# A depthwise convolution in blocks of 32 outputs from 64 inputs, with eight channels side by side in the array, and the key projection moved to the end

## The chip, the cores and the metric

The kernel runs on one core of a Trainium2 chip. The metric is the device time of one execution in microseconds. The kernel before takes 2551.14 us (the median of 3 runs, 2549.97 to 2555.72). A TensorE (PE), a VectorE (DVE), a ScalarE (ACT) and a GpSimd (POOL) compute; SyncE (SP) issues every DMA.

## The reference

The kernel computes a trunk of two layers on x of 1024 tokens by 1024 channels in fp32. Each layer projects x to 9 blocks of 256 columns that feed four mixers, joins the mixers' outputs by an output projection and a LayerNorm, and runs a SwiGLU network with a second LayerNorm. The change touches the first mixer and the order of the last three blocks.

```python
for l in range(2):
    h = x @ w_in[l]                                 # 1024 -> 9 * 256 columns
    a, g = split(h[:, 0:512])                       # mixer A: 256 channels
    z = a * sigmoid(g)
    z = depthwise_conv(z, conf_dw_w[l])             # 31 taps along the tokens, centred
    y_a = silu(layer_norm(z + conf_dw_b[l], conf_ln_g[l], conf_ln_b[l]))
    y_b = s5(h[:, 512:768])                         # mixer B: a state-space scan
    y_c = gate * conv3(c * v)                       # mixer C: h[:, 768:1536]
    q, k, v = split(h[:, 1536:2304])                # mixer D: 4 heads, two softmax maps each
    y_d = diff_attention(rope(q), rope(k), v)
    x = layer_norm(1.414 * x + concat(y_a, y_b, y_c, y_d) @ w_out[l])
    x = layer_norm(1.414 * x + swiglu(x))
```

## The kernel before

**Large matmuls.** Each fp32 product is made of three fp32r products, a high and a low half of both operands (`mm3`). In a layer, blocks of w_in go through a ring of two tiles (`win`); `load_in_block` loads one and splits it. Channel-major blocks are made by `chan_gemm` (tile `cg`), token-major ones by `tok_gemm` (tile `tg`). The nine blocks go in the order of `in_blocks` (line 1513): S5 input, a, g, three for mixer C, then keys, values, queries.

**The convolution.** `conf_a` and `conf_g` leave z channel-major in `zp`. `conv_windows` (line 1068) transposes windows of 128 inputs that step by 96, 11 of them, so that tokens stand on partitions (`zT`, tile `convz`; transposes `cvw`). For each of the 256 channels `conv_part` (line 1083) does one fp32 matmul (`cvo`): 128 inputs on the rows, the channel's 128x96 band of taps as weights, its 11 windows as the moving columns. The bands are read from a table in DRAM (`taps_scr`), nine channels at a time, into a ring of three buffers. DVE adds the bias. `conv_norm` (line 1103) takes mean and variance with `bn_stats`, normalizes, transposes back (`cvb`) and applies gain, bias and SiLU on ACT.

The parts stand among the eight `s5_pair` steps (line 1560). A pair puts eight matmuls (`s5v`) before a chain of DVE operations and six (`s5y`) after it; its tables need matmuls `s5wp` and `s5k`. Mixer C's blocks are spread between the pairs as a list `gem`.

**Attention.** `attn_k` (line 1187) copies a token pair's keys to SBUF (ACT), applies the rotation (POOL, six operations), stacks high and low halves (ACT cast, POOL subtraction), transposes them (`ktp`, eight per token block of 128) and copies them to `kst`. `attn_heads` computes the scores (`sc`) of a query block against all 1024 keys, so the first `sc` needs every `kst`; DVE takes the row's maximum, ACT the exponentials. The four tiles of w_out are split at that time too.

**Order.** Nothing runs in program order. `Weaver` records all operations and sorts them with a list scheduler: it has a cost per operation, a shift in priority per step and layer (`SHIFT`, line 73), and a preference among engines for the operations that may run on any of two or three (`PREF`, line 86). The result is one order per engine, in which that engine then waits in turn. In a profile every operation stands under line 471 (`emit`), so tiles tell them apart. An fp32 matmul that is not a transpose leaves two records on PE, so the 512 convolution matmuls are 1024 records.

Of the kernel before, what the change touches and what calls it, by code (L numbers as in the profile page):

```python
# [9 lines left out]
F32 = mybir.dt.float32  # L10
# [8 lines left out]
P = 128  # L19
# [5 lines left out]
GW = 256  # L25
# [20 lines left out]
R_SW, R_LG, R_LB, R_GB, NROW = 0, 3, 4, 5, 6  # L46


CB, CWIN, NBLK, CG = 96, 128, 11, 9
NCK = -(-GW // CG)  # L50
WROW = CB + CWIN
CBANK = 43
# [16 lines left out]
class Weaver:  # L69
# [3 lines left out]
    SHIFT = {"None": -3232, "attn_finish0": 525, "attn_finish1": -8000, "attn_heads0": 2951, "attn_heads1": -4395,  # L73
# [12 lines left out]
    PREF = {"attn_finish0 gpsimd": -4310, "attn_finish0 scalar": -769, "attn_finish0 vector": 4528,  # L86
# [398 lines left out]
class Trunk:  # L485
# [3 lines left out]
    def __init__(self, ctx, tc, t):  # L489
# [16 lines left out]
        self.ident = self.identr.bitcast(F32)  # L506
        self.mhalf = self.cp.tile([P, 6], F32, name="mhalf")
        nc.vector.memset(self.mhalf, -0.5)
        self.rope = self.cp.tile([P, NJ, 2, 4], F32, name="rope_sb")
        nc.sync.dma_start(self.rope, t["rope"])  # L510


# [1207 lines left out]
```

## Time and profile before

| what | value |
|---|---|
| runs, median of 3 | 2551.14 us (2549.97 to 2555.72) |
| the profiled execution, own time | 2548.31 us |
| its span, first to last instruction | 2546.5 us |
| mean granted TensorE clock | 0.964 of full |
| PE, DVE, POOL, ACT busy | 2438.0, 1592.5, 1243.4, 795.2 us |

The profile gives each engine's busy time and, where an engine was idle, what ended the wait. "PEclk" is the share of full clock that TensorE was granted; in this trace a stretch is at full clock or at half of it (2.4 or 1.2 GHz), and a mean between them is a mix of the two. The mean duration of a matmul is longer than its share of the time, since matmuls overlap; busy time divided by the count is the share.

### The profile page before, as it was taken

The numbers are of one execution on the slowest core, as the hardware profiler recorded it, in microseconds if no ns is written. First come the engines' busy times: TensorE is split into PE (matmuls) and PEld (weight loads), VectorE is DVE, ScalarE is ACT, GpSimd is POOL, SyncE is SP. The second block draws the span as 40 slices with busy tenths as digits, with TensorE's granted clock in tenths as the row PEclk, the third lists the DMA queues.
The fourth block names the chain that finished last, engine by engine and source line by source line (L and its number), as shares of the span: only waits on it lengthen the run. The fifth ranks groups of instructions, "written<-read, shape, count | busy, mean of one in ns | idle before, by whom it ended". The sixth has DMA issues, their size and how long they took to land. (4 is left out here: it accounts for less than half of the span.)

```text
span 2546.5 us, 34450 instructions
## 1 busy us (share of the span) xinstructions
PE 2438.0 (96%) x13464; PEld 2049.7 (80%) x13464; DVE 1592.5 (63%) x2559; ACT 795.2 (31%) x1343; POOL 1243.4 (49%) x1015
## 2 busy tenths in 40 slices
PE   8999989888999999999899999899989999999997
PEld 7889987677888888888688899777778888888885
DVE  6688348886555555555563785698855445554456
ACT  2200356543222222222231113555432222222231
POOL 2201373535566666565640004745376655555574
PEclk9998899999999999999899989999999999999998
DMA  6334321114111111111333342211241111111212
GB/s 165 100 90 132 98 73 51 60 51 155 53 53 55 50 50 58 51 53 55 113 114 85 85 124 91 73 63 55 72 132 58 53 56 52 56 50 50 58 53 96
DMA packets 193081, 193.53 MB, mean 76 GB/s; under 512 B 84878, under 2 KB 168088, under 8 KB 192664
## 3 DMA queue, kind: packets, MB, share of 16 engines
q1 hardware_dynamic: 192920, 191.34, 24.9%
q8 instruction: 106, 1.74, 0.3%
q14 instruction: 55, 0.45, 0.1%
HBM read 164.61 MB, written 26.71 MB: 75 GB/s over the span
## 5 line engine op out<-in xcount | busy, mean ns | idle before, releaser
L471 PE MATMUL up<-xT,wring 128*128 128x512 f32 x2112 | 485.9, 389 | 0.0
L471 PEld LDWEIGHTS up<-xT,wring 128*128 128x128 f32 x2112 | 396.4, 188 | 82.3
L471 PE MATMUL dn<-wring,g 128*128 128x512 f32 x1920 | 450.4, 391 | 3.9 <-POOL wring L471 3.1
L471 POOL TENSOR_TENSOR wring<-upraw,wring 128x512 fp32r<-128x512 f32 x220 | 311.5, 1418 | 250.4 <-ACT wring L471 250.1
L471 PEld LDWEIGHTS dn<-wring,g 128*128 128x128 f32 x1920 | 359.8, 188 | 83.3 <-POOL wring L471 6.6
L471 PE MATMUL up<-xB,wring 128*128 128x512 f32 x1584 | 370.0, 389 | 0.2 <-DVE xT L471 0.2
L471 PEld LDWEIGHTS up<-xB,wring 128*128 128x128 f32 x1584 | 297.3, 188 | 62.1 <-DVE xT L471 0.4
L471 DVE TENSOR_TENSOR r<-r,dn 128x512 f32<-128x512 f32 x288 | 197.9, 687 | 214.0 <-PE dn L471 214.0
L471 ACT CAST wring<-upraw 128x512 fp32r<-128x512 f32 x220 | 136.6, 621 | 469.8 <-PE dn L471 162.5
L471 PE MATMUL cg<-xh,win 128*128 128x512 f32 x640 | 220.9, 414 | 3.1 <-POOL win L471 1.9
L471 PE MATMUL tg<-win,xh 128*128 128x256 f32 x1024 | 203.0, 296 | 1.0 <-POOL win L471 0.6
L471 PE MATMUL wo<-wout,yhl 128*128 128x512 f32 x768 | 195.8, 400 | 0.0
L471 PEld LDWEIGHTS tg<-win,xh 128*128 128x128 f32 x1024 | 170.5, 202 | 3.2 <-POOL win L471 0.9
L471 ACT ACTIVATE probs<-sc,asm 128x1024 f32<-128x1024 f32 x128 | 143.2, 1120 | 91.8 <-DVE asm L471 91.7
L471 DVE TENSOR_REDUCE asm<-sc 128x1 f32<-128x1024 f32 x128 | 155.3, 1217 | 24.7 <-PE sc L471 24.3
L471 PEld LDWEIGHTS wo<-wout,yhl 128*128 128x128 f32 x768 | 142.1, 190 | 28.8 <-POOL yhl L471 0.3
L471 POOL TENSOR_TENSOR wring<-w2raw,wring 128x512 fp32r<-128x512 f32 x80 | 103.7, 1301 | 105.0 <-ACT wring L471 105.0
L471 PE MATMUL tg<-win,xl 128*128 128x256 f32 x512 | 153.2, 300 | 0.0
L471 PEld LDWEIGHTS cg<-xh,win 128*128 128x128 f32 x640 | 126.0, 197 | 32.7 <-issue 2.9
L471 POOL CAST win<-wraw 128x1024 fp32r<-128x1024 f32 x21 | 27.8, 1326 | 212.6 <-PE cg L471 160.1
L471 PE MATMUL cg<-xl,win 128*128 128x512 f32 x320 | 129.5, 405 | 0.0
L471 POOL TENSOR_TENSOR wring<-tw,wring 128x512 fp32r<-128x512 f32 x88 | 122.7, 1394 | 7.8 <-ACT wring L471 7.8
(232 smaller groups left out, 3851.1 us busy)
## 6 DMA issues: line engine op xcount, KB each, us to landing
upraw<-in_w_ffn_dram SPq DMA_DIRECT2D x88, 512.0 KB, 3.8
w2raw<-in_w_ffn_dram SPq DMA_DIRECT2D x44, 512.0 KB, 3.5
wraw<-in_w_in_dram SPq DMA_DIRECT2D x36, 512.0 KB, 4.5
ctap<-taps_scr SPq DMA_DIRECT2D x38, 432.0 KB, 4.9
woraw<-in_w_out_dram SPq DMA_DIRECT2D x16, 512.0 KB, 3.7
r<-x_scr SPq DMA_DIRECT2D x16, 512.0 KB, 4.0
conv<-taps_scr SPq DMA_DIRECT2D x18, 432.0 KB, 4.8
x_scr<-xr SPq DMA_DIRECT2D x14, 512.0 KB, 3.0
```

The source lines that it names most:

```text
L471: getattr(e, method)(*args, **kwargs)
```

## The change

The convolution uses 32 blocks of 32 outputs, each from a window of 64 inputs. Windows of 128 inputs are still transposed, now stepping by 32, and each transpose serves two windows, one on the lower and one on the upper 64 partitions: channels 0 to 63 of a half take the lower rows, 64 to 127 the upper. A channel's matmul has its 64x32 windows as weights and its 64x32 band of taps as moving operand; row half and output column group go round so that eight matmuls in a row take eight places of the array. The taps of 64 channels are read by two DMAs into one buffer, four times per layer. Channels then lie in four groups of 32 partitions per output time, so mean and variance are sums over the free axis followed by a small matmul with a matrix of ones per group (`grp4`), and the transposes back go two output times at a time. `conv_norm` is recorded inside the S5 loop at pair 3. The blocks run values, queries, keys. `SHIFT` and `PREF` have other numbers throughout; two lines of 21 are shown.

```diff
-CB, CWIN, NBLK, CG = 96, 128, 11, 9
+CB, CWIN, NBLK, WROW = 32, 64, 32, 96
...
-            "short_v0": -2551, "short_v1": -1049, "to_xT0": -2061, "token_operands0": 5395, "token_operands1": 2148}
+            "short_v1": 7832, "to_xT0": -5018, "token_operands0": 5383, "token_operands1": 1484}
...
-            pair = int(outs[0].shape[0]) == 64
-            return max(128.0, 0.4167 * 4 * n + 5) * (0.57 if pair else 1.0), 0
+            k, m = int(kw["lhsT"].shape[0]), int(outs[0].shape[0])
+            if k == 64 and m == 32:
+                return 40.0, 0
+            return max(128.0, 0.4167 * 4 * n + 5) * (0.57 if m == 64 else 1.0), 0
...
+        for w0 in range(-2, NBLK, 4):
+            ps = self.b((P, 4, P), "cvw")
+            for i in range(min(4, NBLK - w0)):
+                c0, c1 = CB * (w0 + i), min(CB * (w0 + i) + P, 1040)
+                if c0 < 0:
+                    nc.tensor.matmul(ps[64:P, i, :], lhsT=z[:, c0 + 64:c1], rhs=self.ident, start=True, stop=True)
+                else:
+                    self.tr(ps[0:c1 - c0, i, :], z[:, c0:c1])
+            for h in range(2):
...
+                        nc.scalar.copy(zt[64 * h:64 * h + n, :, x0:x1].rearrange("p c b -> p b c"), src[0:n, i0:i0 + x1 - x0, :])
...
-            for c in range(c0, c1):
-                q, k = divmod(c, CG)
-                tap = self.tring[q % 3]
...
-                nc.tensor.matmul(ps[0:CB, h, (c - c0) * NBLK:(c - c0 + 1) * NBLK], lhsT=tap[:, k * CB:k * CB + CB], rhs=self.zT[:, :, c], start=True, stop=True)
+        for kb in (0, 32):
+            for a in range(2):
+                src = self.wrd[2 * l + ct, 64 * a + kb:64 * a + kb + 1, :]
+                nc.sync.dma_start(self.tapt[64 * a:64 * a + 64], bass.AP(src.tensor, src.offset, [[1, CWIN], [WROW, 32], [1, CB]]))
+            for k in range(kb, kb + 32):
+                j = k % 4
+                for a in range(2):
+                    r = slice(64 * a, 64 * a + 64)
+                    nc.tensor.matmul(ps[32 * j:32 * j + 32, a, k // 4, :], lhsT=self.zT[r, 64 * ct + k, :], rhs=self.tapt[r, k - kb, :],
+                                     start=True, stop=True)
...
+        v.tensor_reduce(st[:, 0], yT_(y), axis=AX.X, op=ALU.add)
+        ps = self.b((P, CB), "cvs")
+        gsum(ps, st[:, 0])
+        nc.scalar.activation(st[:, 1], ps, AF.Copy, scale=1.0 / GW)
+        yv = y.rearrange("p (s t) -> p s t", t=CB)
+        v.tensor_tensor(yv, yv, bc(st[:, 1]), op=ALU.subtract)
+        nc.scalar.activation(q, y, AF.Square)
+        v.tensor_reduce(st[:, 2], yT_(q), axis=AX.X, op=ALU.add)
...
+        nc.gpsimd.tensor_tensor(st[:, 3], st[:, 3], self.cexp, op=ALU.pow)
+        xn = q.rearrange("p (t s) -> p t s", t=CB)
+        v.tensor_tensor(xn.rearrange("p t s -> p s t"), yv, bc(st[:, 3]), op=ALU.mult)
...
-        return [OFF_S5, 0, GW, OFF_SC + GW, OFF_SC + 2 * GW, OFF_SC, OFF_DA + GW, OFF_DA + 2 * GW, OFF_DA]
+        return [OFF_S5, 0, GW, OFF_SC + GW, OFF_SC + 2 * GW, OFF_SC, OFF_DA + 2 * GW, OFF_DA, OFF_DA + GW]
...
         for pr in range(8):
-            if pr % 3 == 0:
-                self.conv_part(l, pr // 3)
+            if pr < 2:
+                self.conv_part(l, pr)
+            elif pr == 3:
+                self.conv_norm(l, yT)
...
-        self.conv_norm(l, yT)
         for jp in range(4):
-            self.attn_k(xT, w(6), jp)
+            self.attn_v(xT, w(6), jp)
         nxt(7)
         for jp in range(4):
-            self.attn_v(xT, w(7), jp)
+            self.attn_q(xT, w(7), jp)
         for jp in range(4):
-            self.attn_q(xT, w(8), jp)
+            self.attn_k(xT, w(8), jp)
```

On PE, at the start of the convolution of layer 0, the order before has the matmuls `cvo` in groups of nine, one group per load of taps, between pieces of mixer C's blocks (`cg`):

```order
L471 MATMUL cvw_164<-ident,conv_118 128x128 x3
L471 MATMUL s5v_166<-s5u_110,s5t_146 64x128 x8
L471 MATMUL cvo_165<-convz_135,ctap_55_136 96x11 x9
L471 MATMUL cvo_165<-convz_135,ctap_56_137 96x11 x9
L471 MATMUL cvo_165<-convz_135,conv_118 96x11 x9
L471 MATMUL cg_177<-xh_4_84,win_89 128x512
```

In the change the same place has `cvo` in groups of 64 (in layer 0 the first is cut into 34 and 30 by eight transposes), here the fourth group of layer 0 with what stands ahead of it, back to the third:

```order
L466 MATMUL cvo_186<-ctap_139,convz_138 32x32 x64
L466 MATMUL cg_197<-xh_5_87,win_91 128x512
...
L466 MATMUL cg_197<-xh_5_87,win_91 128x512
L466 MATMUL s5wp_182<-ident,s5k_149 128x128 x4
L466 MATMUL s5k_183<-s5t_148 48x144 x4
L466 MATMUL s5v_187<-s5u_112,s5t_148 64x128 x8
L466 MATMUL cvo_186<-ctap_139,convz_138 32x32 x64
```

Between the two groups stand 12 `cg`, 4 `s5wp`, 4 `s5k` and 8 `s5v`; a layer has four such groups.

On SP, in layer 0, the loads of taps before alternate with those of the S5 tables (`m_scr`) and of weights:

```order
L471 DMA wraw_203<-in_w_in_dram 128x4x256
L471 DMA ctap_55_136<-taps_scr 128x9x96
L471 DMA ctap_56_137<-taps_scr 128x9x96
L471 DMA m_scr<-s5k_147 16x8x128 x2
L471 DMA s5t_146<-m_scr 128x256
```

In the change the first pair of tap loads stands far ahead, and the other three pairs stand together:

```order
L466 DMA wraw_210<-in_w_in_dram 128x4x256
L466 DMA ctap_139<-taps_scr 64x32x32 x6
L466 DMA m_scr<-s5k_149 16x8x128 x2
L466 DMA s5t_148<-m_scr 128x256
```

Since all loads go into the one buffer `ctap`, each pair waits for the last matmul of the group before it.

On PE, at the first scores (`sc`) of layer 0, the order before still has pieces of the query block (`tg`) around them:

```order
L471 MATMUL tg_272<-win_88,xh_5_85 128x256 x2
L471 MATMUL sc_297<-kst_154_235,stg_234 128x512 x2
L471 MATMUL sc_298<-kst_154_235,stg_234 128x512 x2
L471 MATMUL tg_272<-win_88,xl_7_87 128x256
L471 MATMUL tg_272<-win_88,xh_5_85 128x256 x2
```

In the change the last `tg` is of the key block; half of the layer's key transposes (`ktp`) follow it, and no other block is left when the scores begin:

```order
L466 MATMUL tg_283<-win_90,xl_7_89 128x256
L466 MATMUL ktp_279<-ident,stg_262 128x128 x4
...
L466 MATMUL ktp_288<-ident,stg_262 128x128 x4
L466 MATMUL qtp_306<-ident,stg_262 128x128 x4
L466 MATMUL qtp_307<-ident,stg_262 128x128 x4
L466 MATMUL sc_310<-kst_180_263,stg_262 128x512 x2
```

In layer 0 32 of the 64 `ktp` stand behind the last `tg`, in layer 1 it is 48. The value and query blocks now stand between the S5 pairs.

## Rows read from the trace of the kernel before

**Rows 1.** The page: busy us, share and instructions of each engine

```profile
PE 2438.0 (96%) x13464; PEld 2049.7 (80%) x13464; DVE 1592.5 (63%) x2559; ACT 795.2 (31%) x1343; POOL 1243.4 (49%) x1015
```

**Rows 2.** Two convolution stretches: length, PE PEld DVE ACT POOL busy, PEclk, DMA share, GB/s

```profile
100.00:300.00 200.00, 199.31 (x1369) 179.53 (x1368) 138.12 (x307) 29.10 (x57) 36.31 (x44) 0.87 0.38 102
1375.00:1550.00 175.00, 174.97 (x1218) 155.55 (x1218) 132.16 (x315) 28.48 (x50) 10.81 (x17) 0.87 0.40 107
```

**Rows 3.** Groups of PE: names, shapes, records, then busy us and mean ns

```profile
L471 PE MATMUL cvo<-convz,ctap 128*96 128x11 f32 x700 | 72.7, 245 | 0.0
L471 PE MATMUL po<-aT,vq 128*64 128x128 f32 x1024 | 64.9, 280 | 0.0
L471 PE MATMUL cvo<-convz,conv 128*96 128x11 f32 x324 | 35.2, 248 | 0.0
L471 PE MATMUL cvw<-ident,conv 128*128 128x128 f32 x44 | 6.2, 273 | 0.1
L471 PE MATMUL s5cps<-ident,s5b 16*128 16x16 f32 x64 | 4.2, 207 | 1.0 <-DMA s5b<-in_s_c_re_dram 0.8 <-DMA s5b<-in_s_c_im_dram 0.2
```

**Rows 4.** Timeline of PE, layer 0: start us, length us, what

```profile
114.32 0.39 PE L471 MATMUL s5v<-s5u,s5t 128*64 128x128 f32 x4
114.64 3.23 PE L471 MATMUL cvo<-convz,ctap 128*96 128x11 f32 x36
117.72 1.83 PE L471 MATMUL cvo<-convz,conv 128*96 128x11 f32 x18
...
262.09 2.94 PE L471 MATMUL cvo<-convz,ctap 128*96 128x11 f32 x18
264.88 0.56 PE L471 MATMUL tg<-win,xh 128*128 128x256 f32 x1
```

**Rows 5.** The chain that ended last: one product of 24 records, alone on PE

```profile
1932.18 5.44 PE up L471 x24
```

**Rows 6.** DMA issues: KB each, median us from issue to landing

```profile
ctap<-taps_scr SPq DMA_DIRECT2D x38, 432.0 KB, 4.9
```

**Rows 7.** Busy time of `tg` alone, after each layer's first `sc`

```profile
348.20:366.00 17.80, 11.10 (x87) 10.83 (x85) 0.60 (x1) 1.00 0.31 98
1606.40:1624.00 17.60, 11.13 (x87) 10.83 (x85) 0.60 (x1) 1.00 0.29 96
```

**Rows 8.** Groups of ACT and POOL in the key chain

```profile
L471 ACT CAST stg<-probs 128x512 fp32r<-128x512 f32 x16 | 9.9, 624 | 8.8 <-PE ktp L471 3.7 <-POOL stg L471 3.4 <-POOL probs L471 1.7
L471 ACT CAST kst<-ktp 128x512 fp32r<-128x512 f32 x15 | 8.1, 589 | 4.0 <-PE ktp L471 4.0
L471 ACT COPY probs<-tg 128x512 f32<-128x512 f32 x8 | 4.6, 582 | 4.5 <-PE tg L471 4.5
...
L471 POOL TENSOR_TENSOR stg<-probs,stg 128x512 fp32r<-128x512 f32 x16 | 20.5, 1289 | 21.9 <-ACT stg L471 21.9
L471 POOL TENSOR_TENSOR ropet<-probs,rope_sb 128x64 f32<-128x64 f32 x32 | 10.0, 339 | 173.6 <-ACT probs L471 173.5
L471 POOL TENSOR_TENSOR probs<-ropet 128x64 f32<-128x64 f32 x16 | 5.9, 384 | 0.5
```

**Rows 9.** Stretches: layer 0's first attention block and its third; columns as in Rows 2

```profile
348.20:380.60 32.40, 25.70 (x215) 22.22 (x214) 26.77 (x25) 19.99 (x36) 29.69 (x31) 1.00 0.29 98
406.90:431.40 24.50, 23.36 (x168) 18.44 (x167) 21.88 (x30) 15.76 (x28) 12.65 (x10) 1.00 0.19 61
```

**Rows 10.** Stretches from first `s5v` to last `s5y` of each layer; columns as in Rows 2

```profile
113.60:281.80 168.20, 167.51 (x1165) 151.50 (x1165) 129.83 (x293) 13.96 (x31) 17.71 (x13) 0.85 0.42 111
1375.70:1536.70 161.00, 161.00 (x1134) 144.76 (x1134) 119.59 (x285) 21.75 (x39) 0.00 (x0) 0.86 0.41 108
```

**Rows 11.** Groups of DVE and ACT that are priced by size

```profile
L471 DVE TENSOR_REDUCE asm<-sc 128x1 f32<-128x1024 f32 x128 | 155.3, 1217 | 24.7 <-PE sc L471 24.3
L471 DVE TENSOR_TENSOR convz<-cvo,cbias 96x473 f32<-96x473 f32 (+1 forms) x12 | 11.8, 986 | 24.5 <-PE cvo L471 23.1 <-issue 1.4
L471 DVE BATCH_NORM_STATS2 convz<-convz 96x6 f32<-96x256 f32 x22 | 8.5, 396 | 0.1
```

More of the change, by code (lines that the diff above doesn't have):

```diff
@@ L43 @@
 LN2_LO = -2.12194440e-4
[L46 to L52 removed]
+R_SW, R_GB, NROW = 0, 3, 4
+CB, CWIN, NBLK, WROW = 32, 64, 32, 96
 class Rec:
@@ L1017, in conv_alloc @@
         T = self.convt = self.S([P, SROW], F32, "conv")
-        self.zp = [T[:, c * 1088:c * 1088 + 1088] for c in range(2)]
+        self.zp = [T[:, c * 1040:c * 1040 + 1040] for c in range(2)]
         for z in self.zp:
             self.nc.gpsimd.memset(z[:, 0:16], 0.0)
-            self.nc.gpsimd.memset(z[:, 16 + SEQ:], 0.0)
     def z_half(self, ct, hf):
@@ L1082, in conv_part, with conv_windows @@
[L1082 to L1101 removed]
+    def conv_windows(self, l, ct):
+        nc, t = self.nc, self.t
+        if ct == 0:
+            for i, k in enumerate(("conf_ln_g", "conf_ln_b")):
+                for h in range(2):
+                    nc.sync.dma_start(self.cprm[64 * h:64 * h + 64, i, :], t[k][l].rearrange("(s j) -> s j", j=4))
+            nc.sync.dma_start(self.cbr, t["conf_dw_b"][l].rearrange("(s j) -> j s", j=4))
+            ps = self.b((P, 64), "cbp")
+            nc.tensor.matmul(ps, lhsT=self.sel4.rearrange("p j w -> p (j w)"), rhs=self.cbr, start=True, stop=True)
+            nc.scalar.copy(self.cb, ps)
+        z, zt = self.zp[ct], self.zT[:, 64 * ct:64 * ct + 64, :]
+        for h in range(2):
+            nc.gpsimd.memset(zt[64 * h + 32:64 * h + 64, :, NBLK - 1:], 0.0)
+        for w0 in range(-2, NBLK, 4):
[6 more added lines that the diff above has]
+                    self.tr(ps[0:c1 - c0, i, :], z[:, c0:c1])
+            for h in range(2):
+                b0, b1 = max(0, w0 + 2 * h), min(NBLK, w0 + 2 * h + 4)
+                cut = b1 == NBLK and b0 < b1
+                src = ps[64 * h:64 * h + 64, :, 64 * h:64 * h + 64]
+                for x0, x1, n in ((b0, b1 - cut, 64), (b1 - 1, b1, 48)) if cut else ((b0, b1, 64),):
+                    if x0 < x1:
+                        i0 = x0 - w0 - 2 * h
+                        nc.scalar.copy(zt[64 * h:64 * h + n, :, x0:x1].rearrange("p c b -> p b c"), src[0:n, i0:i0 + x1 - x0, :])
@@ new lines, in conv_part @@
+    @step
+    def conv_part(self, l, ct):
+        nc = self.nc
+        ps = self.d((P, 2, 16, CB), "cvo")
+        for kb in (0, 32):
[8 more added lines that the diff above has]
+                                     start=True, stop=True)
+        y = self.zTt[:, 1024 * ct:1024 * ct + 1024].rearrange("p (a s t) -> p a s t", a=2, t=CB)
+        cb = self.cb[:, 32 * ct:32 * ct + 32].rearrange("p (a s) -> p a s", a=2)
+        for a in range(2):
+            nc.vector.tensor_tensor(y[:, a], ps[:, a], cb[:, a].unsqueeze(2).to_broadcast([P, 16, CB]), op=ALU.add)
@@ L1133, in conv_norm @@
-        for ct in range(2):
-            nc.sync.dma_start(yT[ct].rearrange("p (j c) -> p j c", j=NJ), out[ct])
+        nc = self.nc
+        v = nc.vector
+        yT_ = lambda t: t.rearrange("p (s t) -> p t s", t=CB)
+        y, q, o = self.zTt[:, 0:2048], self.zTt[:, 2048:SROW], self.zTt[:, 2048:SROW]
+        st = self.cst
+        gsum = lambda ps, x: nc.tensor.matmul(ps, lhsT=self.grp4.rearrange("p j w -> p (j w)"), rhs=x, start=True, stop=True)
+        bc = lambda x: x.unsqueeze(1).to_broadcast([P, 64, CB])
@@ new lines, in conv_norm @@
+        v.tensor_reduce(st[:, 0], yT_(y), axis=AX.X, op=ALU.add)
[6 more added lines that the diff above has]
+        v.tensor_reduce(st[:, 2], yT_(q), axis=AX.X, op=ALU.add)
+        ps = self.b((P, CB), "cvs")
+        gsum(ps, st[:, 2])
+        v.tensor_scalar(st[:, 3], ps, 1.0 / GW, EPS, op0=ALU.mult, op1=ALU.add)
@@ new lines, in conv_norm @@
+        nc.gpsimd.tensor_tensor(st[:, 3], st[:, 3], self.cexp, op=ALU.pow)
+        xn = q.rearrange("p (t s) -> p t s", t=CB)
+        v.tensor_tensor(xn.rearrange("p t s -> p s t"), yv, bc(st[:, 3]), op=ALU.mult)
+        o = y.rearrange("p (j e c) -> p j e c", j=4, e=4)
+        for th in range(4):
+            ps = self.b((P, 4, 4, CB), "cvb")
+            for e in range(4):
+                t0 = 8 * th + 2 * e
+                self.tr(ps[:, e].rearrange("p j w -> p (j w)"), xn[:, t0:t0 + 2, :].rearrange("p t s -> p (t s)"))
+            for j in range(4):
+                nc.scalar.activation(o[:, j, :, 3 - th::4], ps[:, :, j, :], AF.Silu, scale=self.cprm[:, 0, j:j + 1], bias=self.cprm[:, 1, j:j + 1])
@@ L1137, in short_c @@
+        for h in range(2):
+            dst = yT[0:2].rearrange("q p (a n) -> (q p) a n", a=NJ)[:, 7 - h::-2, :]
+            nc.sync.dma_start(dst.rearrange("(s j) e n -> s j e n", j=4), o[64 * h:64 * h + 64])
     @step
@@ L1558, in mixers_in @@
         gi = 0
-        self.conv_windows(l)
+        for ct in range(2):
+            self.conv_windows(l, ct)
         for pr in range(8):
-            if pr % 3 == 0:
-                self.conv_part(l, pr // 3)
+            if pr < 2:
+                self.conv_part(l, pr)
+            elif pr == 3:
+                self.conv_norm(l, yT)
             self.s5_pair(pr)
```

84 lines of the change are left out of this document (20 added, 64 removed), and 59 rows, old and new, of tables (PREF, SHIFT).

## The prediction

> **What bounds the kernel now.** I read the page first: PE is busy for 2438.0 of 2546.5 us, and no other engine comes near [rows 1]. So time comes off only if PE gets less work, a higher clock or fewer waits, and the question for each edit is what it does on PE. Second, the busy times by stretch show where PE's time is poorly spent. In the two stretches in which the convolution runs, PE is busy without a break (199.31 of 200, 174.97 of 175), but the granted clock is 0.87 on average [rows 2], against 0.964 over the whole execution. DVE is at 138 and 132 us there, POOL at 36 and 11, so they have room. Third, PE's groups: the convolution's 1024 records take 72.7 + 35.2 = 107.9 us of PE [rows 3], 4% of the kernel, for a product with 11 moving columns. The timeline shows both clocks: 36 records from 114.64 to 117.72, 86 ns each; later 18 records from 262.09 to 264.88, 155 ns each [rows 4]. Last, the start of attention: the first scores are issued while PE still has 11.1 us of projections to do in either layer [rows 7], so that the slow start of the softmax costs PE little now.
>
> The sum is made against the profiled execution, 2548.3 us (span 2546.5); the median of the runs shown is 2.8 us above it, and I add that at the end.
>
> **What the convolution takes now.** At full clock it would be 1024 x 86 ns = 88 us. The mean clock of 0.87 means 0.13 x 200 + 0.13 x 175 = 49 us lost to half clock in the two stretches [rows 2]. Of that, 108 - 88 = 20 us is inside the convolution's own records; the other 29 us are paid by the projections and S5 matmuls beside it. I put all of it down to the runs of narrow convolution matmuls, because the half-clock stretches lie among them [rows 4]. Footprint: 88 + 49 = 137 us.
>
> **What it takes after.** There are again 512 matmuls, 1024 records, each with 32 weight columns and 32 moving columns, in eight places of the array in turn. No row has this shape. The nearest are: 96 weight columns and 11 moving, 105 ns a record; 64 weight columns and 128 moving, in two halves of the array in turn, 64.9/1024 = 63 ns; 16 rows and 16 moving columns, 4.2/64 = 66 ns [rows 3]. The upper bound is that nothing shrinks: 105 ns, 108 us. The lower bound is that eight places share what two share now: 63/4 = 16 ns, 16 us. I take half of the 64-column row, 32 ns, 33 us, since that row is nearest in kind (places in turn) and weight columns halve. For the clock: 49 us lost beside 88 us of such matmuls is 0.56 per us, so 33 us would lose 18; none is the other end. I take 12, since four short groups per layer stand between full-width projections. After: 45 us. Gain: 137 - 45 = **92 us**.
>
> Between the full array and column tiles the trace shows no gap: four `s5v` records start at 114.32 and the convolution follows at 114.64, 80 ns a record [rows 4]. The Trainium skill (TensorEngine Tiling (Array Packing), Key Properties) says that a change of tiling mode drains the array. By that rule each of the eight groups pays twice; with a drain of one `s5v` record's length, 0.3 us, it is 16 x 0.3 = 5 us, an estimate, and the gain would be 87; the trace does not bear it out at this one place.
>
> **What is added on PE.** Window transposes go from 44 to 136; eight are ordinary matmuls with two records, so 100 records more at 6.2/44 = 0.14 us [rows 3]: +14 us. The transposes back fall from 44 to 32, which I leave at nothing. The sums for mean and variance and the bias spread are six small matmuls: +1.
>
> **Taps.** Before, a ring of three buffers hides the loads. Now three loads per layer wait for the previous group's last matmul, and the next group waits for them. A load of 432 KB takes 4.9 us to land [rows 6]; a pair of the new ones is 512 KB, some 5.6 us with a second issue. What covers them on PE is in the order: in the place shown 12 `cg` at 5.44/24 = 0.227 us [rows 5], 2.7 us, and with the S5 matmuls about 5; the six covers are between 4 and 7 us. So about 1 us each: +6 us. Bounds: 0, and 27 if the load takes twice as long (9.8 us against some 5.3 of cover, six times). The S5 table loads queued on SP behind these belong to later pairs, so nobody waits for them at once.
>
> The runs of one load shrink from 384 to 128 bytes, and no row shows loads of taps in such runs. The Trainium skill (DMA: Bandwidth & Descriptors, Specifications) gives 512 bytes as the least for full rate. By that rule the stall lies toward the upper bound just given, not at 6 us.
>
> **The key block last.** This is the edit that costs. The 11.1 us per layer of projections that ran under the start of attention [rows 7] must now be done before the first score: +22 us. They do fill the S5 stage instead, but PE has no holes there to fill. Behind the last key matmul a chain follows that nothing covers: copy 0.58, four rotations at 0.34 and two at 0.38, cast 0.62, two subtractions at 1.29, transposes, two copies at 0.59 [rows 8]: 0.6 + 2.1 + 0.6 + 2.6 + 0.7 + 1.2 = 7.8 us, and with six hand-overs at an estimated 0.2, 9 us. PE spends some 2 us of them on transposes that it has to do anyway, so 7 us in layer 0; in layer 1, where 48 and not 32 transposes stand behind the last matmul, POOL is one pair of subtractions further behind, 9. +16 us, between 4 and 30. In return the first attention block is relieved: it takes 32.4 us against 24.5 for a later one, with POOL busy for 29.7 on splitting w_out [rows 9], which DVE now does before. Much of that excess is the start itself; I take -1 per layer (0 to -8): **-2**.
>
> **What is hidden.** DVE loses the bias additions and `bn_stats` (11.8 + 8.5) and gets eight passes over 2048 elements, at 1217 ns per 1024 [rows 11] some 19.5 us, and shorter additions: no change. Window copies, SiLU and the power on 32 columns load ACT and POOL, idle most of that time [rows 2]. Their cover is the rest of the S5 stage: y_a is needed only by the output projection. The stage from first `s5v` to last `s5y` is 168.2 and 161.0 us with DVE at 129.8 and 119.6 [rows 10]; since the value and query blocks move in as the convolution shrinks, PE stays the longer one. Without these blocks the stage would stop at DVE's 120 to 130, which is why the block order and the convolution belong together. The feed-forward part, where PE runs back to back [rows 5], only has casts moved from ACT to DVE; I cost it at nothing, with 5 us either way.
>
> **Sum:** -92 + 14 + 1 + 6 + 22 + 16 - 2 = -35. 2548.3 - 35 + 2.8 = **2516 us**.
>
> **Rivals.**
> 1. *The narrow matmuls really overlap and the clock stays up.* For it: the 64-column row already takes less than the 96-column one with twelve times the moving columns [rows 3]. Then 16 us, no clock loss, taps and key chain covered: -137 + 16 + 15 + 22 + 4 - 2 = -82, that is 2469. Against it: eight groups of 64 are still narrow work in a row, as what precedes half clock now.
> 2. *Slower: a record's time does not shrink with its width.* One mechanism, on PE in the eight groups: if a record keeps its 105 ns, the groups take 108 us and lose half clock as now (49), the footprint of 137 becomes 157, and the change pays its 57 us of additions for nothing: 2551 + 20 + 57 = 2628. It decides from 33 + 35 = 68 us on, 66 ns a record, which is just what the row of 16-column transposes shows; at that price the time is 2551. Against it: those transposes have 128 weight columns, and 63 ns holds at 64 columns with 128 moving [rows 3].
> 3. *The key chain eats the gain.* If POOL falls behind by two token pairs in both layers and the half clock after the wait reaches into the first block, 15 us more per layer: 2546. For it: POOL does rotation, subtraction and the S5 output there; against it: POOL no longer splits w_out at that time.
>
> That the change does not do what it says would be matmuls standing in eight places but running one after another; its price is rival 2's.
>
> **How the numbers follow.** Forecast 0.64, its own range 2494 to 2540 (record 16 to 50 ns, clock loss 0 to 18, stall 0 to 15); rival 1 0.18; rival 2 0.09, of which a third ends within 5 us of 2551; rival 3 0.09, of which a third each faster, the same and slower. About 0.2% (5 us) is what a measurement of this kernel can tell from no change. Faster: 0.64 + 0.18 + 0.03 = 0.85; same 0.03 + 0.03 = 0.06; slower 0.09. The range takes in most of rival 1 and reaches to no change: 2474 to 2550.
>
> **What would show it.** Right: the convolution's group near 33 us; PEclk in its stretches above 0.93; gaps of about 1 us before three of four groups, ended by the tap load; the first score 15 to 25 us earlier in either layer's count, with some 7 us of idle PE ahead of it, ended by ACT and POOL; attention itself as long as now. Wrong: a convolution group over 60 us, or PE idle in the S5 stage behind DVE, which would mean that DVE and not PE sets it.

## The result and the profile after

The changed kernel takes 2522.61 us (the median of 4 runs, 2517.96 to 2525.68) against 2550.55 for the kernel before, measured beside it: a ratio of 0.989, interval 0.9863 to 0.9918, 28 us less. The profiled execution takes 2517.96 us, its span is 2516.2. It is the quickest of the four, and that of the kernel before is below its median too, so the two traces differ by 30.3 us.

The page, line of the engines:

```profile
PE 2357.2 (94%) x13564; PEld 1957.1 (78%) x13564; DVE 1682.6 (67%) x2586; ACT 801.1 (32%) x1371; POOL 1212.8 (48%) x991
```

Against [rows 1] PE is busy for 80.8 us less, but the span is only 30.3 us shorter: PE is idle for 50.5 us more. The prediction got its time nearly right, and this line says that its reasons can't all have been. Next, PE's groups (columns as in [rows 3]) and the tap loads (as in [rows 6]):

```profile
L466 PE MATMUL cvw<-ident,conv 128*128 128x128 f32 (+2 forms) x144 | 22.6, 281 | 4.2 <-ACT convz L466 3.7
L466 PE MATMUL ktp<-ident,stg 128*128 128x128 f32 x128 | 16.1, 277 | 15.4 <-POOL stg L466 13.9 <-ACT kst L466 1.6
L466 PE MATMUL cvo<-ctap,convz 64*32 64x32 f32 x1024 | 11.1, 200 | 1.1 <-DMA ctap<-taps_scr 1.1
```

```profile
ctap<-taps_scr SPq DMA_DIRECT2D x16, 256.0 KB, 5.3
```

The 1024 records of `cvo` take 11.1 us, 11 ns each, where 107.9 us stood [rows 3] and I forecast 33. PE waited once for taps, 1.1 us. The window transposes (`cvw`) take 22.6 us, and wait 3.7 us for the copies that empty their bank. The key transposes (`ktp`) wait 13.9 us for POOL; in the kernel before they waited for nothing, since other products stood between them. The timeline of PE (start, length) at the second group of layer 0:

```profile
126.99 1.09 PE L466 MATMUL s5v<-s5u,s5t 128*64 128x128 f32 x16
128.01 1.29 PE L466 MATMUL cvo<-ctap,convz 64*32 64x32 f32 x128
129.23 0.50 PE L466 MATMUL cg<-xh,win 128*128 128x512 f32 x1
```

A whole group of 128 records is over in 1.29 us. No gap shows before or behind it, so the drain that the Trainium skill announces (TensorEngine Tiling (Array Packing), Key Properties) costs nothing that shows here.

Stretches, columns as in [rows 2]. First two of the kernel before, layer 0: from the end of the S5 stage to the first `sc`, and from there to the first matmul of the feed-forward part (FFN).

```profile
281.80:348.20 66.40, 65.72 (x528) 61.43 (x528) 8.79 (x33) 36.43 (x61) 42.46 (x56) 0.99 0.20 71
348.20:612.20 264.00, 226.58 (x1568) 184.49 (x1566) 223.91 (x295) 142.21 (x253) 126.19 (x107) 0.95 0.23 79
```

The change, layer 0: S5 stage, from there to the first `sc`, from the first `sc` to the first FFN matmul. Layer 1: S5 stage, to the first `sc`. Then a stretch around each first `sc`, and last the one in which the convolution groups of layer 0 stand:

```profile
127.00:297.60 170.60, 158.37 (x1439) 141.50 (x1439) 146.01 (x277) 30.07 (x61) 43.41 (x36) 0.97 0.24 61
297.60:335.50 37.90, 28.75 (x203) 23.75 (x201) 20.68 (x32) 22.81 (x41) 31.62 (x44) 0.88 0.38 126
335.50:598.70 263.20, 222.67 (x1481) 179.17 (x1481) 220.59 (x302) 138.21 (x243) 98.84 (x82) 0.92 0.21 71
1374.10:1540.60 166.50, 159.05 (x1598) 143.22 (x1598) 137.97 (x289) 37.42 (x68) 28.05 (x39) 0.99 0.26 66
1540.60:1575.20 34.60, 24.34 (x159) 19.07 (x158) 17.67 (x25) 20.59 (x37) 22.16 (x26) 0.81 0.37 120
...
326.40:350.40 24.00, 14.23 (x53) 9.95 (x54) 18.34 (x20) 15.99 (x27) 9.20 (x7) 0.50 0.31 107
1562.10:1589.40 27.30, 14.89 (x61) 10.32 (x60) 26.50 (x36) 17.25 (x29) 17.50 (x13) 0.50 0.40 130
...
118.00:146.00 28.00, 26.27 (x645) 21.35 (x643) 16.73 (x42) 12.60 (x24) 0.00 (x0) 1.00 0.39 62
```

The S5 stages did not get shorter, 170.6 and 166.5 us against 168.2 and 161.0 [rows 10], though the convolution nearly vanished. The clock there went from 0.85 and 0.86 to 0.97 and 0.99, PE is now idle for 12.2 and 7.5 us, and DVE is busy for 16 and 18 us more. The stages also start later (127.0 for 113.6 in layer 0). The gain shows behind them: the value and query blocks were done inside, and the first `sc` follows 37.9 us after the stage and no longer 66.4. It comes at 335.5 for 348.2. In layer 1, counted from the layer's first transposes (1242.8 in the change, 1259.1 before), it comes 14.9 us earlier. Around the first scores a new price stands: 24 and 27 us at half clock. PE is busy for 14.2 and 14.9 us of them, so the clock costs at most some 7 us in each; the rest is waiting. The timeline shows what went ahead of them (the last number in brackets is idle time before, and what ended it):

```profile
322.46 0.79 PE L466 MATMUL ktp<-ident,stg 128*128 128x128 f32 x8
323.88 0.94 PE L466 MATMUL ktp<-ident,stg 128*128 128x128 f32 x8 [0.63 <-POOL stg L466]
330.05 1.25 PE L466 MATMUL ktp<-ident,stg 128*128 128x128 f32 x8 [5.24 <-POOL stg L466]
331.56 1.23 PE L466 MATMUL ktp<-ident,stg 128*128 128x128 f32 x8 [0.26 <-ACT kst L466]
334.09 1.25 PE L466 MATMUL qtp<-ident,stg 128*128 128x128 f32 x8 [1.30 <-POOL stg L466]
335.51 2.08 PE L466 MATMUL sc<-kst,stg 128*128 128x512 f32 x4 [0.17 <-ACT stg L466]
```

PE waits 5.24 us for POOL's subtraction; the granted clock fell at 326.4, inside that wait, and stayed at 1.2 GHz through the first scores. In the S5 stages it was the same: the granted clock is at half from 176.2, 196.6, 220.6 and 1459.6, each time in a wait of PE for DVE of 2 to 4 us or up to 1.5 us behind one. Beside the convolution groups of layer 0 it is full, as the last stretch shows. PE's waits in layer 0's S5 stage (us in total, times, longest) name DVE, as the prediction's last sentence on what would show it wrong had it:

```profile
PE cg L466 <- DVE p L466: 4.1, 1, 4.1
PE s5y L466 <- DVE s5k L466: 4.0, 3, 1.9
PE tg L466 <- DVE sca L466: 2.8, 1, 2.8
```

Why DVE has more to do there is read from its groups. The normalisation has four long passes per layer, two sums, a subtraction and a product:

```profile
L466 DVE TENSOR_REDUCE conv<-convz 128x32 f32<-128x2048 f32 x4 | 15.5, 3877 | 0.5 <-ACT convz L466 0.5
L466 DVE TENSOR_TENSOR convz<-convz,conv 128x2048 f32<-128x2048 f32 x4 | 12.1, 3027 | 4.8 <-POOL conv L466 4.8
```

They take 3.9 and 3.0 us each where the prediction had 2.4, and they stand inside the stage. With the bias additions that is 17 us in layer 0's stage, where the old convolution had 11. The rest of the 16 us are mostly operations that take longer than before; the last experiments come back to them.

### The profile page after: what moved, and what is told of

Read it like the earlier page. It is cut to its first block, busy times and chain, and to the rows that moved or that the text cites. A ratio compares the mean times of both kernels' runs of the same rounds, so it can differ in the third digit from the quotient of the medians.

```text
span 2516.2 us, 34762 instructions
## 1 busy us (share of the span) xinstructions
PE 2357.2 (94%) x13564; PEld 1957.1 (78%) x13564; DVE 1682.6 (67%) x2586; ACT 801.1 (32%) x1371; POOL 1212.8 (48%) x991
## 4 chain that ended last, share of the span: by engine, by line
PE 72%; DVE 15%; POOL 5%; issue 3%; ACT 3%; DMA 2%; SPq 0%; POOLq 0%; DVEq 0%; ACTq 0%
PE up L466 32%; PE dn L466 16%; PE tg L466 6%; PE wo L466 5%; PE cg L466 3%; DVE asm L466 3%; PE po L466 2%; DVE probs L466 2%; DVE s5k L466 2%; PE sc L466 2%; DVE s5t L466 2%; PE atp L466 1%; ACT convz L466 1%; DVE s5w L466 1%; DMA wraw<-in_w_in_dram 1%
## 5 line engine op out<-in xcount | busy, mean ns | idle before, releaser
L466 PE MATMUL cg<-xh,win 128*128 128x512 f32 x640 | 215.1, 404 | 7.1 <-DVE p L466 4.1
L466 PE MATMUL tg<-win,xh 128*128 128x256 f32 x1024 | 195.1, 289 | 3.2 <-DVE sca L466 2.8
L466 PEld LDWEIGHTS tg<-win,xh 128*128 128x128 f32 x1024 | 163.2, 195 | 5.8 <-DVE sca L466 3.2
L466 POOL TENSOR_TENSOR wring<-tw,wring 128x512 fp32r<-128x512 f32 x88 | 129.4, 1470 | 72.7 <-ACT wring L466 72.7
L466 PE MATMUL tg<-win,xl 128*128 128x256 f32 x512 | 147.6, 291 | 0.0
L466 ACT CAST wring<-tw 128x512 fp32r<-128x512 f32 x88 | 54.8, 622 | 241.0 <-PE dn L466 130.1
```

The lines of the kernel that those rows point to most:

```text
L466: getattr(e, method)(*args, **kwargs)
```

## The experiments

Three things change: the convolution, the order of the blocks, and the numbers of `SHIFT` and `PREF`. Five runs and the two kernels take them apart. Every run was measured beside the kernel before, whose median lay between 2548.7 and 2553.8 us, so a difference of less than some 5 us between two runs says nothing. The list scheduler makes a new order for each kernel: leaving `cvo` aside, about 1 PE record in 100 stands elsewhere than in the change when the places are not taken in turn, 1 in 15 with fewer DVE passes or with the splits off POOL, 1 in 9 with the matmuls four times over.

**One part at a time.** Old block order in the changed kernel (with the change's tables, and with the old ones), and the new order in the kernel before:

```diff
 # e1_conv_alone: the changed kernel with
-OFF_DA + 2 * GW, OFF_DA, OFF_DA + GW]   # values, queries, keys
+OFF_DA + GW, OFF_DA + 2 * GW, OFF_DA]   # keys, values, queries; attn_k, attn_v, attn_q called so
 # e9_conv_old_tables: the same, SHIFT and PREF as before
 # e5_old_tables: the changed kernel, SHIFT and PREF as before
 # e2_keys_last_alone: the kernel before with
-OFF_DA + GW, OFF_DA + 2 * GW, OFF_DA]
+OFF_DA + 2 * GW, OFF_DA, OFF_DA + GW]
 # e12_old_conv: the same, SHIFT and PREF as in the change
```

> The change with the blocks in the old order (keys, values, queries), the change's tables kept. Theory K (the key chain is what eats the gain): in the changed kernel PE idles 9 to 10 us ahead of each first score and then runs 24 and 27 us at half clock, which loses another 12 to 13 us; with queries last both go, and the 11 us of projections run under the start of attention again. That is 2 x (9.5 + 12.5) = 44 us less idle and slow time: 2480 to 2495 us. Theory D (DVE sets the S5 stage, and PE waits there for whatever is removed): the values and queries are what fills PE in that stage; without the queries PE idles more there (25 us and more instead of 12 and 7.5), and the first score comes no earlier than now: 2515 to 2530 us.

> The change with the old block order and the numbers of the kernel before in both tables, so that the convolution alone is changed. Theory K: as the first run of this call, 2480 to 2500, if the tables matter little. Theory D: 2515 to 2535, with PE idle over 20 us in each S5 stage. If the tables matter, this and the first run differ by over 10 us.

> The kernel before with the blocks in the order values, queries, keys, its convolution and its tables kept. Theory K: the chain and the half clock behind it cost what they cost in the changed kernel, 2 x 22 us, and the 11 us per layer that ran under attention come on top, since PE has no idle time in the S5 stage: 2551 + 44 + 22 - 2 = 2615, say 2595 to 2620. My prediction's own terms: +22 + 16 - 2 = +36, 2587. Theory D has no cost for the chain itself, only the 22 us that no longer run under attention: about 2570.

> The change with the numbers of the kernel before in both tables. With the old block order the tables made 26 us of difference (2546 with the change's numbers, 2572 with the old). If the tables give the same with the new order, 2540 to 2560. If the order of the blocks alone decides where values and queries go, 2515 to 2530.

> The change with its convolution alone undone: the 96 by 11 matmuls and the norm of before, in the new block order and with the change's tables. So this against the changed kernel is what the convolution is worth in its final place. My sum had the convolution at -92 + 14 + 1 + 6 = -71 us, which gives 2523 + 71 = 2594. Theory of the footprint: 97 us of records and the half clock beside them come back, the window transposes go: 2523 + 126 - 18 = 2631. Theory of tables: the numbers of the change carry most of the gain and the convolution little; then 2540 to 2560.

| convolution | block order | tables | median us | ratio to before, interval |
|---|---|---|---|---|
| old | old | old | (before) | 1 |
| new | old | old | 2572.30 | 1.0081, 1.0051 to 1.0111 |
| old | new | old | 2623.73 | 1.0293, 1.0257 to 1.0329 |
| new | new | old | 2576.48 | 1.0073, 1.0045 to 1.0102 |
| new | old | new | 2546.03 | 0.9971, 0.9954 to 0.9987 |
| old | new | new | 2589.02 | 1.0158, 1.0143 to 1.0174 |
| new | new | new | 2522.61 | 0.9890, 0.9863 to 0.9918 |

No part gains alone. The convolution by itself is 19 us slower (the kernel before took 2553.01 beside it); with the new tables it gains 7. The order alone costs 71. Only beside the other two is the convolution worth much: 2589.0 - 2522.6 = 66 us. (The tables' numbers belong to one form each, so the mixed forms pay for that too; old convolution and old order with the new tables was not run, so what the new tables are worth to the old kernel is not known.) The new convolution with the old order and tables, at 2572, is above both ranges that were given for it; the order alone, at 2624, is above all three of its figures, the prediction's own 2587 among them; the change with old tables, at 2576, is above both of its ranges. All three have the old tables, and the order that these give costs more than was expected. Only the old convolution in the final place came out near a figure: 2594 by the prediction's sum, 2589 measured.

Theory K, that the key chain eats the gain, falls with the first of these runs: PE's wait for POOL ahead of `ktp` falls from 13.9 to 5.2 us, and the time is 2546 and not 2480 to 2495. Theory D had the mechanism, and too little of it (2515 to 2530). The two S5 stages of the new convolution in the old order, with the change's tables, and PE's waits in the first of them, show why:

```profile
129.40:304.30 174.90, 146.50 (x1255) 126.39 (x1254) 147.11 (x277) 28.93 (x59) 48.27 (x44) 0.89 0.23 60
...
1387.50:1555.10 167.60, 142.75 (x1371) 123.34 (x1370) 135.20 (x289) 34.04 (x62) 20.45 (x27) 0.90 0.26 65
```

```profile
PE s5y L466 <- DVE s5k L466: 16.5, 9, 5.4
PE s5wp L466 <- DVE s5k L466: 4.1, 3, 3.3
```

With less to fill it, the stage is as long as ever. PE is idle for 28 and 25 us in it, behind DVE's chain, and the clock is down to 0.89 and 0.90. The convolution groups are the same as in the change, so here half clock comes beside idle time and not beside narrow matmuls. With the old convolution it came while PE was busy without a break [rows 2]; what the two cases have in common was not tried. To keep the clock, the stage needs something else for PE to do once the old convolution is gone.

The price of the order is the key chain, and how much of it depends on the tables. PE's waits for it in the order alone, and in the change with old tables:

```profile
PE ktp L471 <- POOL stg L471: 55.1, 12, 7.8
```

```profile
PE ktp L469 <- POOL stg L469: 52.1, 13, 7.8
```

In the change these waits are 13.9 us, and 16.9 with the old convolution in the same order and tables. In the kernel with old tables layer 0's stretch from the S5 stage to the first `sc` is

```profile
301.10:358.20 57.10, 30.97 (x196) 25.30 (x196) 13.98 (x24) 21.79 (x39) 40.45 (x50) 0.70 0.22 73
```

57.1 us at 0.70 of the clock, where the change takes 37.9 at 0.88. The tables are worth some 50 us in the final form (54 by the medians, 47 by the ratios), and I had looked at them only through the order that they give.

The kernel with the old convolution in the new order and tables is the one that prices my sum. Layer 0's S5 stage, the stretch to the first `sc` and the one from there to the FFN, and its page:

```profile
113.40:284.20 170.80, 167.78 (x1164) 149.54 (x1163) 127.48 (x279) 15.26 (x33) 19.72 (x11) 0.85 0.41 108
284.20:376.50 92.30, 81.36 (x615) 75.67 (x613) 29.07 (x64) 34.69 (x58) 48.40 (x72) 0.91 0.25 87
376.50:629.50 253.00, 223.69 (x1480) 178.40 (x1480) 213.81 (x303) 134.74 (x239) 105.14 (x83) 0.93 0.21 70
```

```profile
PE 2455.7 (95%) x13464; PEld 2059.8 (80%) x13464; DVE 1656.0 (64%) x2643; ACT 754.6 (29%) x1276; POOL 1215.8 (47%) x998
```

From here to the change the S5 stage keeps its length, it starts 13.6 us later, and the stretch behind it falls from 92.3 to 37.9 us: the values and queries moved into the room that the convolution left. PE's busy time falls by 98.5 us, the span (2586.7) by 70.5; 28 us come back as idle time.

**Taking turns over the places.**

```diff
-            for k in range(kb, kb + 32):
-                j = k % 4
-                for a in range(2):
+            for a, j in [(a, j) for a in range(2) for j in range(4)]:
+                for k in range(kb + j, kb + 32, 4):
```

> The change, with the 64 convolution matmuls of a group issued place by place, eight in a row to the same place of the array, instead of taking turns over the eight places. Theory of turns: the 11 ns a record of the changed kernel (11.1 us for 1024) come from neighbours that stand in different places; in a row they run one after another and a record takes something like the 66 to 105 ns that other small matmuls took before, so the group becomes 67 to 108 us and, since PE waits only 20 us in the S5 stages, the time grows by some 35 to 75 us to 2555 to 2600. Theory of width: a record of 32 moving columns is that short wherever it stands; the group stays at 10 to 15 us and the time at 2515 to 2530.

Measured 2545.85 us, ratio 0.9969 (0.995 to 0.9988). The group, a piece of it in layer 0 (60 records in 1.78 us), and the stretch in which the groups of layer 0 stand (columns as in [rows 2]):

```profile
L466 PE MATMUL cvo<-ctap,convz 64*32 64x32 f32 x1024 | 28.8, 194 | 0.0
```

```profile
133.03 1.78 PE L466 MATMUL cvo<-ctap,convz 64*32 64x32 f32 x60
```

```profile
119.40:155.60 36.20, 35.82 (x654) 31.73 (x654) 17.26 (x42) 13.76 (x26) 0.00 (x0) 1.00 0.32 50
```

Both theories are half right. Eight in a row to one place take 28 ns a record, taking turns 11: turns are worth a factor of 2.6, but even without them a narrow record takes a quarter of the 105 ns that it took with 96 weight columns. And 17.7 us more on PE cost some 20 us of time (0.9969 for 0.9890). PE's time is not free in this stage, though PE has idle time there. The clock stayed full beside these slower groups too, so the half clock that the prediction expected from narrow matmuls in a row does not come with this shape, in runs of up to 128 records.

**More on PE, less on DVE.**

```diff
 # e7_four_times: each eight convolution matmuls four times over
+            for k, a in [(k, a) for k0 in range(kb, kb + 32, 4) for _ in range(4) for k in range(k0, k0 + 4) for a in range(2)]:
 # e10_fewer_passes: the sums over y and q, the subtraction and the product
-        v.tensor_reduce(st[:, 0], yT_(y), axis=AX.X, op=ALU.add)
+        v.tensor_reduce(st[:, 0], yT_(y[:, 0:512]), axis=AX.X, op=ALU.add)
```

> The change with every eight convolution matmuls issued four times: the same sums, written four times over, 33 us more of PE work in the S5 stages. If PE sets the end of these stages, 2522 + 33 = 2555. If DVE does (PE idles there 12.2 and 7.5 us, most of it waiting for DVE), the added work takes the place of idle time: +13 or less, 2525 to 2535. If narrow matmuls in a row bring the half clock back, as I had it in the prediction, the added 33 us cost 0.56 x 33 = 18 us on top: 2570.

> The change with the four long passes of the convolution's normalisation on DVE (two sums, a subtraction, a product) over a quarter of the elements only; the rest of the normalisation is left out. That takes 13.9 x 0.75 = 10.4 us of DVE time from each S5 stage and nothing from PE. If PE sets the stage: no change, 2515 to 2530. If DVE sets it: up to 2 x 10 us less, 2502 to 2515.

Four times over: 2605.0 us, 1.0196 (1.0172 to 1.022), more than any theory had. PE did not run the added matmuls through. Its group and a piece of its timeline:

```profile
L466 PE MATMUL cvo<-ctap,convz 64*32 64x32 f32 x4096 | 44.7, 212 | 31.2 <-issue 30.4 <-DMA ctap<-taps_scr 0.7
```

```profile
128.18 0.33 PE L466 MATMUL cvo<-ctap,convz 64*32 64x32 f32 x25
128.70 1.28 PE L466 MATMUL cvo<-ctap,convz 64*32 64x32 f32 x128 [0.19 <-issue]
132.70 1.14 PE L466 MATMUL cvo<-ctap,convz 64*32 64x32 f32 x87 [2.73 <-issue]
```

PE stopped for 30.4 us in 17 places, here after 25 + 128 narrow records, for nothing that the profile shows. So 33.6 us of work took 64 us of PE, and the time grew by 82. Nothing of it went into PE's idle time, as theory D would have it (13 us or less); but with such stalls the run is no clean test of it, and the run by places, where 17.7 us of work cost 20, says the same more plainly. On the clock this run decides nothing, since the stalls stand among the narrow matmuls.

Fewer DVE passes: 2519.17 us, 0.986 (0.9837 to 0.9883), which is not clearly different from the change (0.9863 to 0.9918). Yet the stages did shrink. Layer 0's S5 stage and the stretch to the first `sc`, then layer 1's:

```profile
127.30:289.50 162.20, 154.71 (x1408) 137.30 (x1408) 131.90 (x279) 30.12 (x61) 40.18 (x34) 0.97 0.24 64
289.50:346.70 57.20, 35.43 (x234) 29.76 (x232) 20.13 (x35) 22.04 (x40) 34.36 (x44) 0.75 0.29 100
1375.80:1529.60 153.80, 148.75 (x1524) 132.62 (x1524) 126.87 (x290) 33.52 (x63) 17.33 (x25) 1.00 0.28 71
1529.60:1576.80 47.20, 33.11 (x234) 27.93 (x232) 23.30 (x28) 23.23 (x41) 39.19 (x44) 0.83 0.36 122
```

By 8 and 13 us, as theory D has it; but the stretch behind them grew by 19 and 13, with projections that no longer fitted in and with idle time and half clock in the key chain. Theory D in its plain form falls as well. What these runs agree with is that DVE holds the S5 stage, that PE's work that doesn't fit into it sets the stretch behind, and that the chain's wait comes on top; since the order changed along with the passes, it is argued in part. A gain on DVE alone was given back behind the stage's end.

**Two ways on.** Queries last, so that their products cover the key chain (in both layers, then in layer 0 alone); the splitting of w_in kept off POOL; and both in layer 0:

```diff
 # e3_queries_last; e13_queries_last_l0 in layer 0 alone
-OFF_DA + 2 * GW, OFF_DA, OFF_DA + GW]
+OFF_DA + 2 * GW, OFF_DA + GW, OFF_DA]
 # e11_splits_off_pool, in load_in_block; e14_both: this if l == 0, and e13
-            self.split(raw, t[:, 0, 4 * i:4 * i + 4, :], t[:, 1, 4 * i:4 * i + 4, :])
+            h, lo = t[:, 0, 4 * i:4 * i + 4, :], t[:, 1, 4 * i:4 * i + 4, :]
+            nc.anyp.copy(h, raw)
+            nc.vector.tensor_tensor(lo, raw, h.bitcast(F32), op=ALU.subtract)
```

> The change with values, keys, queries, its tables kept: the last products are the queries', so they stand on PE while POOL rotates and stacks the last keys. Theory K: the wait ahead of the first score falls from 9 to 10 us to 3 or less and the half clock behind it goes: 2480 to 2500 us. Theory D: the same work stands ahead of the first score, so only the idle time of 9 us per layer can be won, and what is done earlier waits for DVE: 2505 to 2520.

> The change with queries last in layer 0 and keys last in layer 1. In the run with queries last in both, layer 0 reached its feed-forward part 7 us sooner than the changed kernel and layer 1 lost 12 us in the S5 stage. If each layer's gain or loss is its own, 2508 to 2517. If the place of the blocks in layer 0 makes no lasting difference (the order of layer 1 follows it), 2518 to 2526.

> The change with the splitting of the weights of w_in kept off POOL: the high half on ACT or DVE, the subtraction on DVE. In the changed kernel DVE operations of layer 0's S5 stage that lie beside POOL's splits take up to six times as long (2.5 us for 0.42), some 25 us in all over that stage. Theory C (this contention holds the stage): DVE gets 9 us of subtractions and loses 25 us of stretching, the stage shortens by 5 to 12 us, 2510 to 2518. Theory P (PE's own work ahead of the first score sets it, as in the run with fewer DVE passes, where the stages got 9 and 13 us shorter and the time 3): no gain, 2518 to 2530. Rival: DVE as the only splitter delays weights: 2530 to 2545.

> The change with queries last in layer 0 and, in layer 0 alone, the splitting of the weights of w_in kept off POOL; layer 1 as in the change. The run with the splits off POOL in both layers began its feed-forward part of layer 0 at 583.1 us, the one with queries last in layer 0 at 591.0, the change at 598.7; from there the change needs 1917.5 us to the end. If the two gains add, 576 + 1917 + 2 = 2495; if they take the same idle time, as the one that gains more alone: 583 + 1917 + 2 = 2502; if the merging of two orders costs what either gained, 2510 or more.

| run | median us | ratio to before, interval |
|---|---|---|
| queries last | 2525.23 | 0.9894, 0.9862 to 0.9927 |
| queries last in layer 0 | 2510.63 | 0.9858, 0.984 to 0.9875 |
| splits off POOL | 2513.03 | 0.9855, 0.984 to 0.987 |
| both, in layer 0 | 2504.31 | 0.9812, 0.9794 to 0.9831 |

Queries last in both layers changes nothing in sum and missed both theories' ranges; in layer 0 alone it is 8 us (by the ratios) to 12 us (by the medians) faster than the change, as the sum by layers had it, though the intervals overlap a little. Why layer 1's S5 stage got 12 us longer with it stays open.

The splits show a cost that I had not seen. On the changed kernel's timeline stand a DVE operation (at two times) and one of POOL:

```profile
139.90 0.42 DVE L466 TENSOR_TENSOR s5k<-s5k,s5t 128x256 f32<-128x256 f32 x1
...
183.08 2.50 DVE L466 TENSOR_TENSOR s5k<-s5k,s5t 128x256 f32<-128x256 f32 x1
```

```profile
182.65 2.65 POOL L466 TENSOR_TENSOR win<-wraw,win 128x1024 fp32r<-128x1024 f32 x1
```

Beside POOL's subtraction the same operation takes 2.50 us for 0.42. The Trainium skill has the rule (SBUF — State Buffer, Who interferes with whom): a DVE instruction with two SBUF inputs contends with a GpSimd instruction that reads SBUF; the trace agrees. Taking for each DVE operation of layer 0's S5 stage what it takes above the quickest quarter of its kind and shape, the sum is 21 us in the change, 13 in the kernel before and 5 with the splits on ACT and DVE. That stage, the one from the first `sc` to the FFN, and layer 1's stretch to its first `sc` then are

```profile
124.20:284.50 160.30, 154.47 (x1445) 138.21 (x1445) 139.18 (x289) 30.60 (x62) 19.64 (x24) 1.00 0.25 65
329.30:583.10 253.80, 222.67 (x1481) 177.47 (x1481) 216.19 (x305) 135.72 (x240) 105.64 (x84) 0.93 0.23 74
1529.20:1566.80 37.60, 22.78 (x135) 17.11 (x133) 19.33 (x25) 19.86 (x36) 23.71 (x22) 0.70 0.38 121
```

The stage is 10 us shorter, and some 10 us of the time go, the number of theory C (the intervals of this run and of the change just overlap). The way there is not all C's. The stretch behind the stage grew by 7 us (to 44.8), so the first score came 6 us sooner (329.3); attention gave 9 more, for a reason that stays open, and the FFN of layer 0 begins 15.6 us sooner (583.1 for 598.7). About half of that is lost again in layer 1, whose first score comes at 1566.8 for 1575.2. Both edits together, in layer 0 alone, are the fastest version, 18 us below the change and clear of its interval. The gains do not add (2495 if they did); 2504 is near what the larger of the two gives alone (2502).

## Why the prediction was right, and where it was not

The time, 2516 forecast and 2522.6 measured, is right, and the two halves of the sum come out near their sizes. The convolution's terms made -71; undone alone it was worth 66. The order's terms made +36; the old convolution in the new order with the new tables takes 40 us more than the kernel before (2548.67 beside it). In part this is luck. Within the convolution's half two errors of some 22 us cancel, as the next two points show. The order's half is right only with the new tables, which the prediction gave no term: with the old ones the order costs 71.

- *The convolution after, 45 us.* Mis-sized. The group takes 11.1 us where I had 33, 11 ns a record for 32 and below my lower bound of 16; the run by places shows that both the width (28 ns in one place) and the turns (11) make it short. The half clock beside it, 12 us in the sum, did not come: the clock is full where the groups stand. By the old convolution in the final place, PE's busy time fell by 98.5 us where the terms -92 + 14 + 1 have 77: some 22 us better, in the direction of rival 1.
- *What is hidden: DVE "no change", and "PE stays the longer one".* This is the step that failed. DVE is busy for 16 and 18 us more in the two stages, by longer passes and by operations that take longer. PE was idle for 19.7 us there where I had none, 18 of them behind DVE. In all 28 us of idle time came between old and new convolution where the sum has 6, so this error of 22 us cancels the first. The prediction set DVE's busy time (120 to 130 us) beside a stage of 168 and called the rest room. The waits show that DVE and PE work in turns there, and with fewer DVE passes the stages got 8 and 13 us shorter. That DVE's chain with its hand-overs was already as long as the stage before the change is not shown, since PE was then busy throughout.
- *Window transposes, +14.* They took 16.4, and 3.7 of waits. *Taps, +6*: 1.1. Loads in 128-byte runs land in 5.3 us for 256 KB against 4.9 for 432 KB before [rows 6], so they are slower by the byte. That is the direction of the 512-byte rule of the Trainium skill (DMA: Bandwidth & Descriptors, Specifications), but the fixed part of a load and the second load of each pair are in the 5.3 too. The stall did not go toward the upper bound, since the covers in the order were enough.
- *Projections, +22, and the key chain, +16.* The idle time ahead of the first scores is 9.2 and 10.3 us, forecast 7 and 9, and POOL's subtractions end it. The half clock behind it (at most some 7 us each) I had only in rival 3. The stretch from the first score to the FFN takes 263.2 us for 264.0 before, as forecast, but not for the forecast's reason: 11 us of projections have left it, and the old convolution in the same order takes 253.0 there. So the +22 was not a net price: with the old convolution attention got 11 and 9 us shorter. What the order costs there is the longer way to the first scores, 92.3 and 89.1 us behind the S5 stages for 66.4 and 69.7.
- *What would show it.* PEclk above 0.93 in the convolution's stretches: yes. The first score 15 to 25 us earlier: 12.7 and 14.9, just short. Gaps before three of four groups: one in all. Of what would show it wrong, PE idle behind DVE did come.
- *The tables.* I cost them at nothing beside the order that they make. With them the chain's waits are 13.9 us rather than 52. Because I read the order of the changed kernel, that was in the numbers without my saying so; a reader who would take over the convolution alone from this prediction would get a slower kernel (2572).
- *Rivals and range.* 1 was right on the convolution's records and clock and wrong on the time; 2, that a record does not shrink, is refuted; of 3 half, the half clock, is there. The three bounds named for the forecast's own range would together reach from 2481 to 2549; 2494 to 2540 leaves out that all of them lie at one end.

## What to carry to other kernels

When work is removed from the engine that is busy, look at what the stage will be bound by without it, and at what can move in: here the convolution gave up 97 us of PE and its stage stayed as long; most of the gain appeared only because other blocks could move in. A second engine that is busy for three quarters of a stage, in turns with the first, may still be the bound. And a right total is no proof of its terms: only undoing one part at a time showed that two errors of some 22 us had cancelled.

## What was not expected of the hardware

- A 64x32 fp32 record of 32 columns takes 11 ns when eight in a row go to eight places of the array, and 28 ns when eight go to one place; 128 records between two other matmuls took 1.29 us, with no gap at either end.
- With the same records four times over, PE stopped among them in 17 places, 30.4 us in all and 0.2 to 3.4 us each, with no releaser in the profile; in the change's groups of 128 it did not. What PE waits for there, and from what length on, was not tried.
- Half clock came behind idle time here, and not beside the new narrow matmuls: the S5 stages of the new convolution in the old order had 0.89 and 0.90 with 28 and 25 us idle, with values and queries to fill them 0.97 and 0.99, and the stretches of the convolution groups 1.00. The old convolution had 0.87 with PE busy throughout.
- A DVE operation with two SBUF inputs took six times as long beside a POOL subtraction (2.50 us for 0.42).
